# The half swap of q moved to ScalarE's queue, and a longer filler for the last attention head

## The chip, the cores and the metric

The kernel runs on one core of a Trainium2 chip. Its measure is the time of one execution on the device in microseconds (us). The engines are TensorE (PE; its weight loads are listed as PEld), VectorE (DVE), ScalarE (ACT), GpSimd (POOL) and SyncE (SP). Each works through its own list of instructions in order, and semaphores tie the lists together. DMAs are issued from the lists of SyncE, ScalarE and GpSimd.

## The reference

The model is a two-layer (DEPTH = 2) diffusion backbone on 512 latent tokens and 256 context tokens of width 1024, in float32. Each layer projects the normalised tokens with one wide matrix `w_in`, mixes them in three branches, and adds a feed-forward network with a width-3 convolution:

```
z = modulate(rmsnorm(x, norm1_g), sh1, sc1) @ w_in            # 512 + 256 tokens
a: v = layernorm(gelu(z[V]));  y_a = gelu(z[U]) * (w_s @ v + b_s)      # spatial gating, 4 halves of 128 columns each
b: q, k = rope(rmsnorm(z[Q])), rope(rmsnorm(z[K]))            # 8 heads, two maps of 64 dims each
   p = softmax(q0 k0^T) - lam * softmax(q1 k1^T);  y_b = rmsnorm(p @ v)
c: y_c = gb * dwconv3(gc * xin)                                # short convolution
x = x + g1 * ((g_a*(y_a @ wa) + g_b*(y_b @ wb) + g_c*(y_c @ wc)) @ wo)
x = x + g2 * conv_ffn(modulate(rmsnorm(x), sh2, sc2))
```

In layer 0 latent and context tokens are both carried on (768 tokens, attention of the context among itself). In layer 1 the context gives keys and values alone, and everything else runs on the 512 latent tokens.

## The kernel before, in words

Every product with a weight matrix is split: `x = hi + lo`, with `hi` rounded to TensorE's fast 4-byte format and `lo` the rest, and three matmuls (hi*hi, lo*hi, hi*lo; lines 183, 184 and 186, in `gemm`) add up in PSUM. Tokens lie along the free dimension, in segments of 512 and (layer 0) 256. A weight tile of 128 x 1024 is called a half. `Stream` brings the halves in the order in which they are asked for: a load on SyncE's queue (line 62, `wraw`, two buffers), the rounding on ScalarE (line 83, `whi`), the remainder on VectorE (line 69, `wlo`). While the attention runs, `late` is set: `wlo` is not issued with `whi` but by `tick`, after each step of the weave.

The order of the instructions is written out by Python generators. `weave` takes several of them, each with a stated total cost; each yield gives the cost of the step, and the generator whose done share of its total is smallest goes next (ties to the first). So a total that is larger than the sum of the yields makes a generator run ahead of the other one and end early; a total equal to the sum spreads it over the other's whole length.

**One head.** `project(h)` computes q, k and v of head h, normalises q and k and applies the rotation. `turn(h)` then weaves `qk_tr` with one half of filler (`fill(1)`, from `c_fill`) and ends with `v_tr`. `attn(h)` is woven with `project(h + 1)`.

**`qk_tr`** works in three chunks of 256 tokens (in layer 1, k alone in the third). For each chunk it transposes q on TensorE into a PSUM tile (line 738), copies that to `qT[:, 0]` on ScalarE (line 741), and starts two DMAs within SBUF (lines 743 and 744): they copy partitions 0 to 63 of `qT[:, 0]` to partitions 64 to 127 of `qT[:, 1]`, and the other way round. q and k are stored as hi and lo parts above each other (64 + 64 partitions), so that with the swapped copy two matmuls give all four products of the parts. Then it does the same for k: transposes (line 738), and two copies by ScalarE to `kT[0]` and `kT[1]` (line 747). The PSUM pool `mm` has four buffers during the attention; the transposes' tiles, the filler's accumulators and `v_tr`'s tiles take turns in them.

**`scores`** (line 857) multiplies one block of 128 tokens of q with all keys, for both maps a: first `qT[:, 0]` (v = 0), then `qT[:, 1]` (v = 1). VectorE takes the minima (lines 861 and 864, `mn`), ScalarE the exponentials (line 869, `pa`), which also frees the score's PSUM buffer; there are two of these, so the next block's map a waits for this block's exponential of map a. `combine` (VectorE) joins the two maps, `to_at` transposes them (line 893) and splits them into `ah` (ScalarE, line 897) and `al` (VectorE, line 898), and `av` (lines 905 to 907) multiplies with v; ScalarE copies the result to `yb` (line 908). `attn_costs` states 20,000 for these steps in layer 0 and 16,000 in layer 1.

**The last head** has no next projection. It is woven with `fill(99)`: what is left of `c_fill`. The nine halves of branch c are used up by then, so this is the `N_VS` = 2 halves of the gating branch's v, each with yields of 2.6 per token and quarter (7,987 in layer 0, 5,325 in layer 1), with a stated total of `(1 + N_VS) * 10000` (layer 0) or `* 6000` (layer 1). They are only copied out to SBUF (line 842, tags B0 and B7).

**After the attention** `branch_a` is woven with `subln` (totals `62000 - 7800 * N_VS` and 20,000):

```
for v in vg: nc.scalar.activation(v[:, :n], v[:, :n], AF.Gelu_apprx_tanh)   # line 1058
for i in range(N_VS, 4): pv = self.fm(("vs", l, i)); ... Gelu ...; yield 7800  # line 1063
ugate(0); yield 7800          # a half of u on TensorE, gelu on ScalarE
... transposes of vg, layer norm ...; ugate(1); yield 7800
for g in range(4): ... mixing with w_s ...; if g + 2 < 4: ugate(g + 2); yield 7800
```

`subln` first squares five heads (ScalarE line 953, hi part line 170, lo part on VectorE line 171; yield 3700), then sums the eight heads' squares on TensorE (line 968, yield 700 each, squaring three more heads on the way), reads the sums on VectorE (line 973, `srs`, yield 1500), and transposes them on TensorE (line 977) for the reciprocal root (yield 3500).

Of the kernel before, what the change touches and what calls it, by code (L numbers as in the profile page):

```python
# [11 lines left out]
F32 = mybir.dt.float32  # L12
# [8 lines left out]
NL, NC, T, D = 512, 256, 768, 1024  # L21
# [9 lines left out]
N_HALF = 2 * (NH * 3 + 12 + 4 + 4 + 24 + 8 + 8 + 8 + 44 + 24)  # L31
N_ADA = 4 * 24
N_LAST = 3
N_VS = 2


def weave(*gens, tick=lambda: None):
    act = [[g, 0.0, float(tot)] for g, tot in gens]
    while act:
        act.sort(key=lambda e: e[1] / e[2])  # L40
        e = act[0]
        try:
            e[1] += next(e[0])
        except StopIteration:
            act.remove(e)
        tick()
# [83 lines left out]
class Net:  # L130
# [34 lines left out]
    def tick(self, n):  # L165
        for _ in islice(self.bg, n):
            pass
# [555 lines left out]
    def qk_tr(self, l, h, pool, st):  # L723
        nc = self.nc
        qT = pool.tile([128, 2, 2, T], F32R, tag="qT", bufs=1, name="qT")
        kT = [self.slots.tile([128, T], F32R, tag=f"B{1 + a}", name="kT") for a in range(2)]
        y = self.qk_rope(l, 2, pool, st)
        yield 1500
        for c in range(3):
            qs, ks = st.pop(("rope", c))  # L730
            t0 = c * 256
            for v, src in enumerate((qs, ks)):
                if src is None:
                    continue
                pt = self.mm.tile([128, 512], F32R, tag="mm", name="mmT")
                for a in range(2):
                    for b in range(2):
                        nc.tensor.transpose(pt[:, (2 * a + b) * 128:(2 * a + b + 1) * 128], src[:, 2 * b + a, :], self.identr)
                pf = pt.bitcast(F32)
                if v == 0:  # L740
                    nc.scalar.copy(qT[:, 0, :, t0:t0 + 256], pf.rearrange("p (a t) -> p a t", a=2))
                    for i, j in ((0, 64), (64, 0)):
                        nc.sync.dma_start(qT[i:i + 64, 1, :, t0:t0 + 256].bitcast(F32),
                                          qT[j:j + 64, 0, :, t0:t0 + 256].bitcast(F32))
                else:
                    for a in range(2):
                        nc.scalar.copy(kT[a][:, t0:t0 + 256], pf[:, 256 * a:256 * a + 256])
            if c == 0:
                st["rope", 2] = self.qk_hl(*y, pool)
            yield 1700  # L750
        st["q"], st["k"] = qT, kT
# [44 lines left out]
    def c_fill(self, l, pool, scr):  # L796
        nc = self.nc
        segs = self.segs
        n = sum(s[1] for s in segs)
        pc = self.pc[l]  # L800

        def half(b, i, evac, kind="c", mid=None):
            w = self.ws.take(kind, l, b, i) if kind == "c" else self.ws.take(kind, l, i)
            for o, m, _ in segs:
                ps = self.mm.tile([128, 512], F32, tag="mm", name="mm")
                for q in range(4):
                    self.gemm(w, [2 * q, 2 * q + 1], self.h, ((o, m, 0),), (ps,), first=(q == 0), last=(q == 3))
                    if mid and q == 2:
                        mid((o, m, 0))
                    if q == 3:  # L810
                        if o == segs[-1][0]:
                            self.ws.ahead()
                        evac(o, m, ps)
                    yield 2.6 * m

        def mul(dst):
            def f(o, m, ps):
                nc.vector.tensor_tensor(dst[:, o:o + m], dst[:, o:o + m], ps[:, :m], ALU.mult)
            return f

        ps = self.cp

        def first(i):
            ps[i] = self.slots.tile([128, T], F32, tag="B7", name="cp")
            return half(1, i, lambda o, m, q: nc.scalar.copy(ps[i][:, o:o + m], q[:, :m]))

        for i in range(4):
            if i > 1:
                yield first(i)
            if i:  # L830
                yield half(2, i, mul(ps[i]))
            c = pool().tile([128, T], F32, tag="cc", bufs=1, name="cc")

            def conv(seg):
                self.conv(c, ps[i], [pc[:, PC_CW + 4 * j + i:PC_CW + 4 * j + i + 1] for j in range(3)], None, [seg])
            yield half(0, i, mul(c), mid=conv)
            nc.sync.dma_start(scr[i][:, :n], c[:, :n])
        self.vg = []
        for i in range(N_VS):
            v = self.slots.tile([128, T], F32, tag=("B0", "B7")[i], name="vg")  # L840
            self.vg.append(v)
            yield half(0, i, lambda o, m, q: nc.scalar.copy(v[:, o:o + m], q[:, :m]), "vs")

# [202 lines left out]
    def branch_a(self, l, pool):  # L1046
# [10 lines left out]
        for v in vg:  # L1057
            nc.scalar.activation(v[:, :n], v[:, :n], AF.Gelu_apprx_tanh)
        for i in range(N_VS, 4):
            pv = self.fm(("vs", l, i))  # L1060
# [190 lines left out]
    def run(self):  # L1251
        tc, nc, d = self.tc, self.nc, self.d
# [8 lines left out]
        def run(g):  # L1261
            for _ in g:
                pass

        with tc.tile_pool(name="const", bufs=1) as const, tc.tile_pool(name="w", bufs=1) as wp, \
# [45 lines left out]
            for l in range(2):  # L1311
# [12 lines left out]
                with tc.tile_pool(name="attn", bufs=1) as ap, tc.tile_pool(name="pmm", bufs=4, space=PSUM) as self.mm, \  # L1324
                        tc.tile_pool(name="ps", bufs=2, space=PSUM) as self.sp:
                    self.ws.late = True
                    st = [dict(h=h) for h in range(8)]
                    tick = self.ws.low

                    def fill(count):  # L1330
                        while count:
                            g = next(cgen, None)
                            if g is None:
                                return
                            yield from g
                            count -= 1

                    chalf = 7800 if l == 0 else 5200

                    def project(h):  # L1340
                        yield from self.qk_proj(l, h, ap, st[h])
                        vp = self.v_proj(l, h, ap, st[h])
                        yield next(vp)
                        if l:
                            st[h]["kc"]()
                            yield next(vp)
                        if h == 0:
                            self.attn_lam(l, ap, tabs[0])
                        self.qk_norm(l, h, ap, st[h])
                        yield next(vp)  # L1350
                        yield next(vp)
                        y = self.qk_rope(l, 0, ap, st[h])
                        yield next(vp)
                        st[h]["y1"] = self.qk_rope(l, 1, ap, st[h])
                        st[h]["rope", 0] = self.qk_hl(*y, ap)
                        yield next(vp)
                        st[h]["rope", 1] = self.qk_hl(*st[h]["y1"], ap)
                        yield from vp

                    def turn(h):  # L1360
                        weave((self.qk_tr(l, h, ap, st[h]), 6800), (fill(1), chalf), tick=tick)
                        run(self.v_tr(l, h, ap, st[h]))

                    p0 = project(0)
                    for i in range(8):
                        if gb:
                            next(gb)
                        next(p0)
                        tick()
                        if i == 5:  # L1370
                            self.attn_setup(l, ap, *tabs)
                    weave((p0, 15000), (fill(1), chalf), tick=tick)
                    turn(0)
                    for h in range(8):
                        a = self.attn(l, h, ap, st[h]), sum(self.attn_costs(l))
                        if h < 7:
                            weave(a, (project(h + 1), 23500), tick=tick)
                            turn(h + 1)
                        else:
                            weave(a, (fill(99), (1 + N_VS) * (6000 if l else 10000)), tick=tick)  # L1380
                self.ws.low()
                self.ws.late = False
                mmp = psum_all()
# [3 lines left out]
                with tc.tile_pool(name="yk", bufs=16) as yk:  # L1387
# [8 lines left out]
                    with tc.tile_pool(name="tmpa", bufs=1) as tmp:  # L1396
                        pp = PP(tmp)
                        weave((self.branch_a(l, pp), 62000 - 7800 * N_VS), (self.subln(l, pp), 20000))
                    with tc.tile_pool(name="tmpb", bufs=1) as tmp:
# [171 lines left out]
```

## Time and profile before

| | us |
|---|---|
| median of 3 runs | 2674.5 (2672.96 to 2675.52) |
| profiled execution | 2675.01 |
| its span, first to last instruction | 2673.2 |
| TensorE busy | 2617.0 (98% of the span) |
| VectorE busy | 1631.2 (61%) |
| ScalarE busy | 1035.2 (39%) |
| mean granted clock of TensorE | 0.993 of 2.4 GHz |

The profile is of one execution. Matmuls overlap, and their ends are modelled, so a busy TensorE may still lose time between matmuls. A wait is put down to whatever was finished last. Start times in the rows below are microseconds from the start of the span. In a timeline row that stands for several instructions, the time is from the first one's start to the last one's end.

### The profile page before, as it was taken

To read this page: it belongs to the slowest core of one execution; us is meant where nothing else is said; L and a number is where in the kernel's file an instruction comes from. 1 tells how busy PE (TensorE), PEld (TensorE's weight loads), DVE (VectorE), ACT (ScalarE), POOL (GpSimd) and SP (SyncE) were. 2 spreads that over 40 slices of the span, in tenths; PEclk is the share of its full clock that TensorE was granted. 3 is DMA by queue.
4 is the path that set the end of the run, shared out by engine and by line. 5 is a ranking of instruction groups with operands and counts; after the bars stand their busy time and mean duration, and the time that the engine had idled before them with its cause. 6 is when DMAs were issued, how large, how long until landed. Compare 5 with 4: busy or idle time off the path is not lost.

```text
span 2673.2 us, 37362 instructions
## 1 busy us (share of the span) xinstructions
PE 2617.0 (98%) x15128; PEld 2267.7 (85%) x15128; DVE 1631.2 (61%) x2887; ACT 1035.2 (39%) x1840; POOL 220.9 (8%) x202
## 2 busy tenths in 40 slices
PE   7999999999999999999999999999999999999999
PEld 3899999888888888888888878898978888888887
DVE  5677777656546447544544567777767564654544
ACT  3455555542121224312312335555563232343422
POOL 0000000001111111100100100000001121010101
PEclk8999999999999999999999999999999999999999
DMA  5212221224333332222222232212125554233233
GB/s 224 82 44 58 64 66 44 66 66 149 113 116 111 103 127 66 76 87 72 79 81 77 91 100 67 68 55 63 53 75 173 175 163 175 71 99 100 94 103 110
DMA packets 79660, 254.36 MB, mean 95 GB/s; under 512 B 9200, under 2 KB 19712, under 8 KB 79104
## 3 DMA queue, kind: packets, MB, share of 16 engines
q1 hardware_dynamic: 64512, 196.64, 23.1%
q0 software_dynamic: 14544, 55.07, 6.4%
q8 instruction: 119, 1.95, 0.3%
q14 instruction: 53, 0.43, 0.1%
q10 hardware_dynamic: 432, 0.27, 0.0%
HBM read 234.63 MB, written 6.82 MB: 90 GB/s over the span
## 4 chain that ended last, share of the span: by engine, by line
PE 82%; DVE 10%; ACT 4%; DMA 2%; issue 1%; SPq 0%; POOL 0%; ACTq 0%; POOLq 0%; DVEq 0%
PE mm L183 22%; PE mm L186 22%; PE mm L184 22%; PE S L857 3%; PE mm L647 2%; PE mm L649 2%; PE mm L648 2%; DVE wlo L69 2%; PE mmT L893 1%; ACT whi L83 1%; DMA qT<-qT 1%; ACT pa L869 1%; DVE zs L697 1%; DVE al L898 1%; PE mmT L906 1%
## 5 line engine op out<-in xcount | busy, mean ns | idle before, releaser
L183 PE MATMUL mm<-hh,whi 128*128 128x512 f32 (+1 forms) x2392 | 855.3, 358 | 12.1 <-ACT hh L376 10.2
L184 PE MATMUL mm<-hl,whi 128*128 128x512 f32 (+1 forms) x2392 | 820.0, 353 | 4.4 <-DVE hl L379 4.1
L186 PE MATMUL mm<-hh,wlo 128*128 128x512 f32 (+1 forms) x2392 | 752.6, 353 | 1.6 <-DVE wlo L69 1.6
L183 PEld LDWEIGHTS mm<-hh,whi 128*128 128x128 f32 x2392 | 452.6, 189 | 104.5 <-ACT hh L376 14.4
L69 DVE TENSOR_TENSOR wlo<-wraw,whi 128x1024 fp32r<-128x1024 f32 x320 | 399.4, 1249 | 195.8 <-ACT whi L83 194.2
L184 PEld LDWEIGHTS mm<-hl,whi 128*128 128x128 f32 x2392 | 453.3, 190 | 68.4 <-DVE hl L379 9.3
L186 PEld LDWEIGHTS mm<-hh,wlo 128*128 128x128 f32 x2392 | 415.1, 190 | 42.1 <-DVE wlo L69 3.7
L83 ACT CAST whi<-wraw 128x1024 fp32r<-128x1024 f32 x320 | 335.0, 1048 | 285.0 <-PE mm L184 243.4
L1018 DVE SCALAR_TENSOR_TENSOR cv<-mm,pc,cv 128x511 f32<-128x511 f32 (+1 forms) x132 | 86.8, 658 | 181.7 <-ACT cv L1017 180.8
L869 ACT ACTIVATE pa<-S,mn 128x768 f32<-128x768 f32 (+1 forms) x160 | 129.3, 813 | 153.1 <-DVE mn L864 125.7
L183 PE MATMUL mm<-ah,whi 128*128 128x512 f32 (+1 forms) x528 | 187.9, 356 | 0.0
L647 PE MATMUL mm<-whi,hh 128*128 128x256 f32 x640 | 183.0, 286 | 1.3 <-DVE cp L794 0.8
L648 PE MATMUL mm<-wlo,hh 128*128 128x256 f32 x640 | 180.7, 282 | 0.0
L649 PE MATMUL mm<-whi,hl 128*128 128x256 f32 x640 | 180.6, 282 | 0.0
L184 PE MATMUL mm<-al,whi 128*128 128x512 f32 (+1 forms) x528 | 179.9, 354 | 0.0
L186 PE MATMUL mm<-ah,wlo 128*128 128x512 f32 (+1 forms) x528 | 161.7, 355 | 0.0
L1017 ACT ACTIVATE cv<-mm,pc 128x512 f32<-128x512 f32 (+1 forms) x132 | 88.7, 705 | 177.2 <-PE mm L186 177.2
L1179 DVE SCALAR_TENSOR_TENSOR x<-mm,mod,x 128x512 f32<-128x512 f32 (+1 forms) x91 | 58.2, 659 | 139.0 <-PE mm L186 139.0
L1222 POOL TENSOR_TENSOR cv<-cv 128x768 f32<-128x768 f32 (+1 forms) x44 | 91.9, 2088 | 607.3 <-DVE cv L1020 420.7
L857 PE MATMUL S<-kT,qT 128*128 128x512 f32 x576 | 118.2, 341 | 10.1 <-DMA qT<-qT 8.7
L647 PEld LDWEIGHTS mm<-whi,hh 128*128 128x128 f32 x640 | 121.9, 190 | 4.3 <-ACT cp L792 1.0
L864 DVE TENSOR_REDUCE mn<-S 128x1 f32<-128x768 f32 x128 | 116.1, 949 | 10.3 <-PE S L857 10.3
(237 smaller groups left out, 4035.9 us busy)
## 6 DMA issues: line engine op xcount, KB each, us to landing
wraw<-w SPq DMA_DIRECT2D x320, 512.0 KB, 3.6
araw<-ada POOLq DMA_DIRECT2D x80, 512.0 KB, 4.0
qT<-qT SPq DMA_DIRECT2D x80, 128.0 KB, 3.8
araw<-ada SPq DMA_DIRECT2D x16, 512.0 KB, 8.3
x<-xT SPq DMA_DIRECT2D x8, 384.0 KB, 7.7
srow<-sscr POOLq DMA_DIRECT2D x3, 1024.0 KB, 5.5
x<-xT POOLq DMA_DIRECT2D x8, 384.0 KB, 6.2
xscr<-x SPq DMA_DIRECT2D x8, 256.0 KB, 3.9
```

Source lines behind the costliest of these rows:

```text
L69: self.lo_eng.tensor_tensor(lo, raw, hi.bitcast(F32), ALU.subtract)
L83: self.nc.scalar.copy(hi, raw)
L183: nc.tensor.matmul(ps[:, :m], lhsT=hh, rhs=xh[:, o:o + m], start=st, stop=False)
L184: nc.tensor.matmul(ps[:, :m], lhsT=hh, rhs=xl[:, o:o + m], start=False, stop=False)
L186: nc.tensor.matmul(ps[:, :m], lhsT=hl, rhs=xh[:, o:o + m], start=False, stop=sp)
L647: nc.tensor.matmul(ps[:, :256], lhsT=hh[:, sl], rhs=hi[:, c:c + 256], start=(k == 0), stop=False)
L648: nc.tensor.matmul(ps[:, :256], lhsT=hh[:, sl], rhs=lo[:, c:c + 256], start=False, stop=False)
L649: nc.tensor.matmul(ps[:, :256], lhsT=hl[:, sl], rhs=hi[:, c:c + 256], start=False, stop=(k == 7))
L857: nc.tensor.matmul(s[:, c0 + o:c0 + o + m], lhsT=st["q"][:, v, a, t0:t0 + 128], rhs=st["k"][a][:, k0 + o:k0 + o + m], start=(v == 0), stop ...
L864: nc.vector.tensor_reduce(mn[:, a:a + 1], ss[a], AX.X, ALU.min)
L869: nc.scalar.activation(pa[:, :nk], ss[a], AF.Exp, bias=mn[:, a:a + 1], scale=-1.0, accum_out=sm[a])
L1222: nc.gpsimd.tensor_tensor(cs[1][:, :n], cs[1][:, :n], cs[0][:, :n], ALU.mult)
```

## The change

The two DMAs of the swap are issued from ScalarE's queue and not from SyncE's. A third half of the gating branch's v goes into the last head's filler (and into slot B2, which holds `kT[1]` before) and leaves `branch_a`. The filler's stated total is set to `N_VS * 10.4` per token, which is the sum of its yields: 23,962 in layer 0 and 15,974 in layer 1. Since `branch_a`'s total depends on `N_VS`, that falls from 46,400 to 38,600.

```diff
-N_VS = 2
+N_VS = 3
...
                 if v == 0:
                     nc.scalar.copy(qT[:, 0, :, t0:t0 + 256], pf.rearrange("p (a t) -> p a t", a=2))
                     for i, j in ((0, 64), (64, 0)):
-                        nc.sync.dma_start(qT[i:i + 64, 1, :, t0:t0 + 256].bitcast(F32),
-                                          qT[j:j + 64, 0, :, t0:t0 + 256].bitcast(F32))
+                        nc.scalar.dma_start(qT[i:i + 64, 1, :, t0:t0 + 256].bitcast(F32),
+                                            qT[j:j + 64, 0, :, t0:t0 + 256].bitcast(F32))
                 else:
                     for a in range(2):
                         nc.scalar.copy(kT[a][:, t0:t0 + 256], pf[:, 256 * a:256 * a + 256])
...
         for i in range(N_VS):
-            v = self.slots.tile([128, T], F32, tag=("B0", "B7")[i], name="vg")
+            v = self.slots.tile([128, T], F32, tag=("B0", "B7", "B2")[i], name="vg")
...
-                            weave(a, (fill(99), (1 + N_VS) * (6000 if l else 10000)), tick=tick)
+                            weave(a, (fill(99), N_VS * 10.4 * (512 if l else 768)), tick=tick)
```

## Rows read from the trace of the kernel before

**Rows 1.** From the page: busy time in us, share of the span and instructions of each engine.

```profile
PE 2617.0 (98%) x15128; PEld 2267.7 (85%) x15128; DVE 1631.2 (61%) x2887; ACT 1035.2 (39%) x1840; POOL 220.9 (8%) x202
```

**Rows 2.** The view of waits, TensorE alone, over the whole span: who waited for whom, us in total, times, longest.

```profile
PE S L857 <- DMA qT<-qT: 8.7, 7, 1.5
...
PE mmT L905 <- ACT ah L897: 4.3, 3, 3.2
...
PE mmT L738 <- ACT qT L741: 1.5, 3, 0.5
```

**Rows 3.** Single lines of the kernel. The first two are of the swap (line 743): length of an issue in ns (min/median/max), first and last start, and then us from issue to landing. The next is of the loads of `pc` (line 1287), which ScalarE's queue issues. The last two are ScalarE's timeline at the start of the program (start us, us, engine, line, operation): a DMA issue and the instruction behind it.

```profile
L743 SPq DMA_DIRECT2D qT<-qT x80: 590/605/1403, 117.1 to 1957.0; - x80
...
DMA to landing us min/median/max: 2.3/3.8/5.5
...
L1287 ACTq DMA_DIRECT2D pc<-pcol x2: 335/335/335, 7.1 to 8.3; - x2
...
0.74 0.41 ACTq L1269 DMA_DIRECT2D cc<-cc  x1
...
1.18 1.28 ACT L1271 ACT_TABLE_LOAD   x1 [1.18 <-PEq L1566]
```

**Rows 4.** Timeline of one turn of layer 1 (head 6), SyncE's queue and then TensorE: start us, us, engine, line, operation, out<-in, form, count, and in brackets the engine's idle time before and what ended it.

```profile
1909.26 0.33 SPq L62 DMA_DIRECT2D wraw<-w  x1
...
1909.77 2.57 SPq L743 DMA_DIRECT2D qT<-qT  x4
...
1915.08 1.29 PE L857 MATMUL S<-kT,qT 128*128 128x512 f32 x6 [1.04 <-DMA qT<-qT]
```

**Rows 5.** Timeline of one turn of layer 0, ScalarE: the copies of q and k of the three chunks, the split of the next weight half, and the exponentials of the first two score steps.

```profile
378.55 0.58 ACT L741 CAST qT<-mmT 128x512 fp32r<-128x512 f32 x1
...
379.02 0.66 ACT L747 CAST kT<-mmT 128x256 fp32r<-128x256 f32 x2
...
381.06 0.41 ACT L716 CAST qs<-ry 128x256 fp32r<-128x256 f32 x1 [1.38 <-DVE ry L708]
...
382.15 0.65 ACT L747 CAST kT<-mmT 128x256 fp32r<-128x256 f32 x2
...
383.64 0.69 ACT L747 CAST kT<-mmT 128x256 fp32r<-128x256 f32 x2
...
384.17 1.10 ACT L83 CAST whi<-wraw 128x1024 fp32r<-128x1024 f32 x1
...
388.64 0.90 ACT L869 ACTIVATE pa<-S,mn 128x768 f32<-128x768 f32 x1 [1.68 <-DVE mn L864]
...
393.61 0.90 ACT L869 ACTIVATE pa<-S,mn 128x768 f32<-128x768 f32 x1 [1.89 <-DVE mn L864]
```

**Rows 6.** The same turn of layer 0: one row of VectorE (the minima of the first score step) and three of TensorE (k's transposes of the third chunk, the second and the third score step).

```profile
387.66 1.81 DVE L864 TENSOR_REDUCE mn<-S 128x1 f32<-128x768 f32 x2
...
382.86 0.54 PE L738 MATMUL mmT<-identr,ks 128*128 128x128 f32 x4
...
390.41 1.57 PE L857 MATMUL S<-kT,qT 128*128 128x512 f32 x8
...
394.68 1.83 PE L857 MATMUL S<-kT,qT 128*128 128x512 f32 x8
```

**Rows 7.** Line 738 (the transposes of q and k), whole span, from its list of what TensorE's weight loads and matmuls waited for there: releaser, us, times. The second row is ScalarE's timeline of the first turn of layer 0.

```profile
  ACT kT L747: 1.2, 8
...
123.14 0.86 ACT L780 CAST vh<-mmT 128x512 fp32r<-128x512 f32 x2 [1.07 <-PE mmT L778]
```

**Rows 8.** Timeline of the turn of Rows 4 and of the score steps behind it: ScalarE, VectorE, TensorE.

```profile
1910.12 0.41 ACT L719 CAST ks<-ry 128x256 fp32r<-128x256 f32 x1 [0.83 <-DVE ry L708]
...
1912.14 1.06 ACT L83 CAST whi<-wraw 128x1024 fp32r<-128x1024 f32 x1
...
1916.72 0.90 ACT L869 ACTIVATE pa<-S,mn 128x768 f32<-128x768 f32 x1 [2.35 <-DVE mn L864]
...
1921.69 0.90 ACT L869 ACTIVATE pa<-S,mn 128x768 f32<-128x768 f32 x1 [1.89 <-DVE mn L864]
...
1915.74 1.81 DVE L864 TENSOR_REDUCE mn<-S 128x1 f32<-128x768 f32 x2
...
1919.08 1.57 PE L857 MATMUL S<-kT,qT 128*128 128x512 f32 x8
...
1923.35 1.56 PE L857 MATMUL S<-kT,qT 128*128 128x512 f32 x8
```

**Rows 9.** Busy time by stretch (stretch, its length, then each engine's busy us with its instructions, granted clock, DMA share and GB/s): the end of the last head of layer 0 and of layer 1.

```profile
519.00:530.00 11.00, 6.51 (x35) 5.26 (x33) 5.56 (x15) 4.10 (x13) 0.64 (x2) 0.84 0.16 48
...
1981.50:1987.50 6.00, 4.44 (x31) 3.70 (x30) 2.01 (x5) 2.91 (x7) 0.74 (x2) 1.00 0.30 90
```

**Rows 10.** Timeline behind the attention: for layer 0 ScalarE's gelu of a gating half straight from TensorE, VectorE's low part of the first square, and VectorE's reading of the sums of squares; for layer 1 the gelu and the low part of the first square.

```profile
538.17 0.87 ACT L1063 ACTIVATE vg<-mm 128x512 f32<-128x512 f32 x2 [4.87 <-issue]
...
540.68 0.96 DVE L171 TENSOR_TENSOR sql<-ssq,sqh 128x768 fp32r<-128x768 f32 x1 [5.72 <-ACT sqh L170]
...
560.61 1.01 DVE L973 TENSOR_SCALAR srs<-ssum 8x512 f32<-8x512 f32 x2 [4.75 <-PE ssum L968]
...
1992.51 0.60 ACT L1063 ACTIVATE vg<-mm 128x512 f32<-128x512 f32 x1 [2.49 <-issue]
...
1994.31 0.69 DVE L171 TENSOR_TENSOR sql<-ssq,sqh 128x512 fp32r<-128x512 f32 x1 [2.63 <-ACT sqh L170]
```

## The prediction, made before the result was known

> **What bounds the kernel now.** I read the page first: TensorE is busy for 2617.0 of 2673.2 us [rows 1], so only 56 us are to be had, and what the other engines do counts only where TensorE waits for it. The view of waits then shows the three places that the change touches: seven waits for the swap's DMA, 8.7 us in all; four waits behind `ah` and `qT`, where the attention's own chain is late [rows 2]. Third I took the timelines of one turn in each layer, to see who has slack. In layer 1 SyncE issues a 512 KB weight load at 1909.26 and the four swap DMAs from 1909.77 on, behind it in one queue; the scores with `qT[:, 1]` go on only at 1915.08, 5.3 us after the first issue [rows 4], against a shortest landing of 2.3 [rows 3]. In layer 0 nothing waits for the swap. There the list of line 738 shows eight waits for the k copies (`kT`), one for each of the eight turns [rows 7]: the third chunk's k transposes need the PSUM buffer of the second chunk's. In the turn shown the copies end at 382.15 + 0.65 = 382.80 and the transposes start at 382.86 [rows 5, 6]. So ScalarE has no slack in layer 0's turns.
>
> **Part 1: the swap on ScalarE's queue.** Removed: SyncE's 80 issues. SyncE's other work (weight loads, stores of `cscr`) is not held up by them at present, so that gives nothing. Added: 80 issues in ScalarE's list, two behind each q copy, each waiting for that copy to end; queued behind them are the k copies, the filler's evacuations, the next `whi`, `vh` and the exponentials.
>
> The price of one issue on ScalarE stands in no row for this shape. From above: the same DMA holds SyncE 605 ns. From below on ScalarE: a DMA of another shape takes 335 ns [rows 3]. Below that still: nothing, if ScalarE's engine went on with its next copy meanwhile. A row speaks against nothing: the table load starts at 1.18, right behind the end at 0.74 + 0.41 = 1.15 of an issue ahead of it [rows 3], but that is one case. I take 605 ns, since the shape is the same: a pair costs 2 x 0.605, about 0.1 for two semaphores and gaps, and 0.11 by which the k copy overlaps the q copy now (379.13 against 379.02 [rows 5]): 1.4 us a chunk.
>
> The Trainium skill, "Perfetto Trace Analysis", section "DMA Instruction — HWDGE (DVE, Sync)", has the issuing sequencer free for its next instruction only when the descriptors are generated, and the profiled time cover just that. By it the sum is the one below; by an issue that blocks nothing it would be rival C. One row agrees, none settles it.
>
> *Layer 0, the turn shown.* First chunk: ScalarE idles 1.38 before 381.06 [rows 5], which absorbs the 1.4. Second chunk: the k copies move from 382.15 to 383.6, so TensorE's third k transposes move from 382.86 to 384.3, and TensorE with them: +1.4. Third chunk: the k copies are late by both pairs, 383.64 to 386.4, and so `whi`, 384.17 to 387.0. From there the chain is VectorE's `wlo`, `vl`, the minima (387.66 to 390.4 [rows 6]) and the exponentials, 388.64 to 391.4. The first exponential ends at 389.54 and the second score step starts at 390.41: slack 0.87. TensorE arrives there at 391.8 and waits until 392.3: +1.9. The same chain runs on through the next weight split to the next exponential, 393.61 + 0.90 = 394.51, and the third score step starts at 394.68: slack 0.17. So that step is late by 2.8 - 0.17, 2.6 us, and TensorE never gets it back. In the first turn ScalarE idles another 1.07 before `vh` [rows 7]: 1.7. Layer 0: 7 x 2.6 + 1.7 = 20 us. With 335 ns an issue a chunk is 0.85 (0.67 + 0.07 + 0.11): 7 x 1.5 + 0.7 = 11. With issues that block nothing: 0.
>
> *Layer 1, the turn shown.* Two chunks swap. ScalarE idles 0.83 before 1910.12 [rows 8], so 0.6 of the first pair and 1.4 of the second remain: `whi` 1912.14 to 1914.1. I let 0.4 of these 2.0 be absorbed before the minima (no row here for it): they start at 1917.3 rather than 1915.74, the exponential at 1918.3 rather than 1916.72, ending at 1919.2. The swap, issued a microsecond earlier and no longer behind the load, has landed by the time of the scores, so TensorE saves its wait, about 1.3 with what is lost around the 1.04, less 0.5 because k's third transposes come later. It reaches the second score step at 1918.3, waits until 1919.2, and is where it was (1919.08). The next exponential ends at 1921.69 + 0.90 + 1.6 = 1924.2, and the third score step starts then instead of at 1923.35: +0.85. Eight heads: 7 us slower. What is late next is thus the exponential, in the place of the DMA. Bounds: -10 (seven waits of 8.7 in all, with the restart, go and nothing comes) and +13 (1.6 a head).
>
> **Part 2: the filler.** TensorE's work stays: the third half has as many matmuls in the filler as in `branch_a`. Now the filler's two halves are used up at 15,974 of a stated 30,000, about half-way, and the attention's end runs bare. In layer 0 TensorE idles 11.00 - 6.51 = 4.5 us there, and the granted clock is 0.84, part of the stretch at 1.2 GHz, some 1.5 us more; in layer 1 it idles 1.6 [rows 9]. With filler up to the last step both go, but for the copy of the last accumulator, 0.5 each: -5.5 and -1. The thinner filler (1.8 pieces a step in layer 0 for 2.25, 1.1 for 1.3 in layer 1) leaves the early score steps less cover; I put +1 on that.
>
> But `branch_a` loses what it gives. With a total of 38,600 its one remaining v half counts 7,800/38,600 = 0.202, more than the 3,700/20,000 = 0.185 of `subln`'s first yield, so the first sum of squares now follows at once on the half, behind which the squares are only started: in ScalarE's order they stand behind the half's gelu. In layer 0 that gelu starts at 538.17 and the first low part ends at 540.68 + 0.96 = 541.64: TensorE waits 3.6, where now a whole half covers it. Layer 1: 1992.51 to 1995.0, so 2.5 [rows 10]. And the sums (`srs`, 1.01 [rows 10]) now stand right between the last sum and their transposes: +1.3 and +1. Costs 4.9 and 3.5, gains 5.5 and 1, thinner filler 1: +3 us. Bounds: -6.5 (all of the cover kept) and +9 (the bare end replaced by other waits).
>
> **Sum.** On the profiled execution's 2675.0 (span 2673.2, 1.8 around it): 20 + 7 + 3 = 30, so 2705. The median shown is 0.5 lower: 2704.
>
> **Rivals.**
> *B: the issue is cheaper.* 335 ns as in ScalarE's own row [rows 3]. Layer 0 +11; in layer 1 only 0.85 is left of a hold, the DMA waits go and the exponentials stay within their slack of 1919.08 - 1917.62: -8; filler +3. 2675 + 6, so 2681.
> *C: faster. ScalarE's engine goes on while its queue issues.* Then no k copy is late, the seven waits of rows 2 and the restarts go (-10), and with +3 for the filler the time is 2668; with a filler that costs nothing 2665. For it: 8.7 us are really there, and ScalarE is busy 39% of the time. Against: the table load that starts on the issue's heels. It decides at the first pair: if the k copy behind an issue starts before the issue's end, C holds.
> *D: nothing moves.* The swap's transfers still share the DMA engines with the weight load and land as late as now (up to 5.5 [rows 3]), and the issues are small enough for ScalarE's idle times. Then only the filler's +3: 2678. Against: the swap alone has landed in 2.3. The Trainium skill, "DMA: Bandwidth & Descriptors", section "Issuing engines are not separate DMA queues", says that transfers interleave on the same 16 engines whoever starts them, and that another issuer saves only issue time, small beside the transfer; this is that rule, and the late landing of rows 4 goes with it, the 1.2 us a pair do not look small here.
>
> **How the numbers follow.** Forecast A 0.60 (2692 to 2712, from 1.7 to 2.8 a turn in layer 0 and from 0 to +13 in layer 1), B 0.10, C 0.22, D 0.08. This kernel's runs tell 0.2%, 5.3 us, from no change: faster is below 2669, slower above 2680. C lies below that bound with 0.16 and within with 0.06; D within with 0.05 and above with 0.03; B above: faster 0.16, same 0.11, slower 0.73. The range goes from 2666 to 2712: it leaves out the lower half of C and the upper end of A.
>
> **What would show it.** On the path: ScalarE's timeline in a layer 0 turn with two issues of about 0.6 between q copy and k copy, and k copies 1.4 later (C: no delay). TensorE's waits for `kT` at line 738 grow from 1.2 to over 10 us, those for `pa` at line 857 from 1.4 to over 10, those for the swap's DMA vanish. One layer 0 head takes 2.6 longer. Behind the attention TensorE waits for `sql` once in each layer, 2.5 to 3.6 us; the idle time of rows 9 is gone. The forecast is wrong if an issue takes under 0.3 or blocks nothing, or if the score steps keep their distance to the exponentials.

## The result, and the profile after

The changed kernel takes 2710.3 us (median of four runs, 2709.5 to 2710.8) against 2675.0 for the kernel before beside it: a ratio of 1.0133, 95% interval 1.0119 to 1.0147, so 35 us slower. The forecast was 2704, slower, with a range of 2666 to 2712.

The page of the kernel after: busy time and share of the span (2708.9 us) by engine, and the engines' shares of the chain that ended last.

```profile
PE 2631.9 (97%) x15128; PEld 2274.4 (84%) x15128; DVE 1630.8 (60%) x2887; ACT 1036.6 (38%) x1842; POOL 220.4 (8%) x202
...
PE 74%; DVE 13%; ACT 8%; DMA 2%; ACTq 2%; issue 1%; SPq 0%; DVEq 0%
```

TensorE is 14.9 us busier than in [rows 1] with the same 15,128 matmuls. The other 20.8 of the span's 35.7 us are idle time. Part of the 14.9 is the clock: the mean granted clock fell from 0.993 to 0.990 over the span, which is some 8 us at full speed (an estimate from these rounded figures: 0.010 x 2708.9 less 0.007 x 2673.2). `ACTq`, ScalarE's issuing, now has 2% of the chain. The waits tell where TensorE stood (TensorE alone, whole span: us in total, times, longest).

```profile
PE S L857 <- ACT pa L869: 14.5, 26, 1.8
...
PE mmT L738 <- DVE ks L720: 4.4, 7, 1.5
...
PE ssum L968 <- ACT sqh L170: 4.3, 2, 2.4
PE ssum L977 <- DVE srs L973: 4.1, 2, 2.8
PE mmT L738 <- DVE cc L818: 4.1, 3, 1.4
PE mmT L738 <- ACT kT L747: 2.9, 2, 1.5
...
PE S L857 <- DMA qT<-qT: 0.2, 1, 0.2
```

The swap's own wait has gone from 8.7 to 0.2 us [rows 2]. In its place the score steps wait 14.5 us for the exponentials, k's transposes wait for ScalarE's copies and for VectorE's `ks` and `cc`, and behind the attention there are two new waits for squares and two for sums.

The list of the swap after (length of an issue in ns, first and last start; us to landing):

```profile
L743 ACTq DMA_DIRECT2D qT<-qT x80: 597/616/1748, 115.4 to 1983.4; - x80
...
DMA to landing us min/median/max: 2.3/2.5/5.6
```

An issue costs ScalarE 616 ns, where SyncE paid 605 [rows 3]. The landing is better, 2.5 for 3.8, but these are medians over both layers; in layer 1, where every swap meets a weight load, it is 3.6 for 4.3. The turn of [rows 5, 6] after the change, ScalarE and then TensorE:

```profile
393.15 0.59 ACT L741 CAST qT<-mmT 128x512 fp32r<-128x512 f32 x1
393.77 1.27 ACTq L743 DMA_DIRECT2D qT<-qT  x2
395.08 0.65 ACT L747 CAST kT<-mmT 128x256 fp32r<-128x256 f32 x2 [1.34 <-PE mmT L738]
...
402.72 0.90 ACT L869 ACTIVATE pa<-S,mn 128x768 f32<-128x768 f32 x1 [2.05 <-DVE mn L864]
...
407.69 0.90 ACT L869 ACTIVATE pa<-S,mn 128x768 f32<-128x768 f32 x1 [1.88 <-DVE mn L864]
```

```profile
395.78 0.53 PE L738 MATMUL mmT<-identr,ks 128*128 128x128 f32 x4 [1.45 <-ACT kT L747]
...
403.76 0.50 PE L857 MATMUL S<-kT,qT 128*128 128x512 f32 x1 [0.30 <-ACT pa L869]
...
408.74 0.85 PE L857 MATMUL S<-kT,qT 128*128 128x512 f32 x3 [0.26 <-ACT pa L869]
```

The k copy begins at 395.08, behind the end of the pair of issues at 395.04. The bracket behind it ("1.34 <-PE") names TensorE, but the row above shows ScalarE's own queue in that time. TensorE pays twice: 1.45 us before the third k transposes, and then from these to the third score step 408.74 - 395.78 = 12.96 instead of 394.68 - 382.86 = 11.82 [rows 6], another 1.14. Together 2.6 us in this turn.

### The profile page after: what moved, and what is told of

It reads as the page before. It is cut to its first block, busy times and chain, and to the rows that moved or that the text cites. A ratio compares the mean times of both kernels' runs of the same rounds, so it can differ in the third digit from the quotient of the medians.

```text
span 2708.9 us, 37309 instructions
## 1 busy us (share of the span) xinstructions
PE 2631.9 (97%) x15128; PEld 2274.4 (84%) x15128; DVE 1630.8 (60%) x2887; ACT 1036.6 (38%) x1842; POOL 220.4 (8%) x202
## 4 chain that ended last, share of the span: by engine, by line
PE 74%; DVE 13%; ACT 8%; DMA 2%; ACTq 2%; issue 1%; SPq 0%; DVEq 0%
PE mm L183 21%; PE mm L186 21%; PE mm L184 21%; PE S L857 2%; DVE wlo L69 2%; ACT whi L83 2%; ACT pa L869 2%; PE mm L647 2%; PE mm L649 2%; PE mm L648 2%; ACTq L743 2%; PE mmT L893 1%; DVE mn L864 1%; ACT kT L747 1%; DMA wraw<-w 1%
## 5 line engine op out<-in xcount | busy, mean ns | idle before, releaser
L857 PE MATMUL S<-kT,qT 128*128 128x512 f32 x576 | 123.3, 348 | 15.0 <-ACT pa L869 14.5
L648 PEld LDWEIGHTS mm<-wlo,hh 128*128 128x128 f32 x640 | 122.1, 191 | 0.9 <-DVE wlo L69 0.8
```

The source lines that it names most:

```text
L648: nc.tensor.matmul(ps[:, :256], lhsT=hh[:, sl], rhs=lo[:, c:c + 256], start=False, stop=False)
L857: nc.tensor.matmul(s[:, c0 + o:c0 + o + m], lhsT=st["q"][:, v, a, t0:t0 + 128], rhs=st["k"][a][:, k0 + o:k0 + o + m], start=(v == 0), stop ...
```

## The experiments

Each is an edit of the kernel before, unless it says otherwise. Changes in us are the ratio's, on 2675; the brackets behind a ratio are its 95% interval.

**The swap alone** (the `nc.scalar.dma_start` lines of the change, nothing else).

> The swap on ScalarE's queue, the filler as before (two halves, old total). Theory (each chunk holds ScalarE for 1.3 us, and the k copies, the weight split and the exponentials behind it end later than TensorE can wait): the forecast's 20 us in layer 0 and 7 in layer 1, so +27, 2702; with the starts of the heads in the changed kernel's trace (layer 0's eight turns +17 to +18, layer 1's +8 to +9) +26. Rival (the loss is the filler's, the swap alone saves its DMA waits): about 2666 to 2675.

2703.2 us, ratio 1.0104 (1.0088 to 1.0119), 28 us. The waits for `pa` at line 857 are 13.3 us.

**The filler alone** (the other lines of the change, the swap on SyncE's queue).

> The third half and the new total, the swap on SyncE's queue as before. Theory by the forecast: +3, 2678. By the changed kernel's trace, where the waits behind the two attentions (first sum of squares, then the sums' transposes) and the clock's fall after them come to some 11 us against 8 gained at the attentions' ends: +3 to +9, 2678 to 2684. Rival (cover is only moved, or the filler gains): 2668 to 2675.

2681.9 us, ratio 1.0028 (1.0018 to 1.0038), 7.5 us; its ten runs spread from 2677.5 to 2688.6. The two parts add up within their intervals: 0.0104 + 0.0028 = 0.0132 for the measured 0.0133. The first mixing with `w_s` (line 1101) is a mark behind the attention and the sums of each layer. Its matmuls before the change, with the swap alone, with the filler alone, and with both (ns min/median/max, first and last start; layer 0, layer 1):

```profile
L1101 PE MATMUL mm<-wst,vt x48: 270/275/377, 572.1 to 595.0; 128*128 128x128 f32 x48
...
L1101 PE MATMUL mm<-wst,vt x32: 270/275/377, 2014.7 to 2030.2; 128*128 128x128 f32 x32
```

```profile
L1101 PE MATMUL mm<-wst,vt x48: 270/275/377, 591.7 to 614.5; 128*128 128x128 f32 x48
...
L1101 PE MATMUL mm<-wst,vt x32: 270/275/377, 2045.1 to 2060.6; 128*128 128x128 f32 x32
```

```profile
L1101 PE MATMUL mm<-wst,vt x48: 272/275/377, 571.8 to 594.6; 128*128 128x128 f32 x48
...
L1101 PE MATMUL mm<-wst,vt x32: 270/275/582, 2020.0 to 2037.6; 128*128 128x128 f32 x32
```

```profile
L1101 PE MATMUL mm<-wst,vt x48: 270/275/377, 590.9 to 613.7; 128*128 128x128 f32 x48
...
L1101 PE MATMUL mm<-wst,vt x32: 270/275/582, 2049.7 to 2067.2; 128*128 128x128 f32 x32
```

By the first mark the swap costs 591.7 - 572.1 = 19.6 us in layer 0; by the second, 30.4, so another 10.8 in layer 1. The filler costs -0.3 and 5.6. The traces with both and with the filler alone give the swap once more: 590.9 - 571.8 = 19.1 us, and 29.7 by the second mark, so another 10.6. (From the second mark to the span's end the four have 658.5, 659.0, 659.3 and 659.2, so little is left out. The swap alone was 2.7 us slower in its profiled execution than in its median, 2705.9 for 2703.2, so its two shares together are up to that much too large.)

**The swap on ScalarE's queue in layer 1 alone.**

```diff
-                        nc.sync.dma_start(qT[i:i + 64, 1, :, t0:t0 + 256].bitcast(F32),
+                        (nc.scalar if l else nc.sync).dma_start(qT[i:i + 64, 1, :, t0:t0 + 256].bitcast(F32),
```

> The swap on ScalarE's queue in layer 1 alone, nothing else changed. Theory: layer 1 has a wait to save (8.7 us in seven waits) and still loses, because the exponential takes the DMA's place: +7 by the forecast, +8 by the trace, 2682 to 2683. Rival (only layer 0, which had no wait for the swap, loses; layer 1 gains what its waits were): 2665 to 2667.

2687.1 us, ratio 1.0046 (1.0031 to 1.0061), 12 us, although the wait for the swap's DMA is gone here too: it is paid back with more for `pa` and, at k's transposes, for `ks` (0.2 before). The rival's gain did not come. TensorE's waits:

```profile
PE S L857 <- ACT pa L869: 9.4, 19, 1.7
...
PE mmT L738 <- DVE ks L720: 4.8, 8, 1.3
```

The listed waits are only part of the 12 us. From layer 1's first transposes to those of its last head, 320.5 us before and 329.8 here, TensorE's idle time grows by 3.5 us and its busy time by 5.8 for the same 2184 matmuls, at the same mean clock of 0.99: much of the loss stands inside the recorded times of matmuls, the score step's (line 857) by 2.6. The two stretches, before and here (length, busy us of TensorE, its weight loads, VectorE, ScalarE, GpSimd; granted clock; DMA):

```profile
1631.20:1951.70 320.50, 310.90 (x2184) 283.88 (x2185) 243.01 (x487) 176.91 (x397) 0.00 (x0) 0.99 0.21 61
...
1631.55:1961.37 329.82, 316.69 (x2184) 284.67 (x2185) 243.00 (x487) 176.12 (x397) 0.00 (x0) 0.99 0.20 59
```

**The swap on GpSimd's queue** (`nc.gpsimd` in its place), which has nothing in its list behind it during a turn.

> The swap issued from GpSimd's queue, nothing else changed: off SyncE's queue and not in ScalarE's way. Theory (the wait of layer 1 comes from the weight load ahead in the same queue, and the loss from ScalarE's time): the seven waits go, nothing comes: -9 to -10, 2665. Rival 1 (the transfers share the DMA engines and land as late as before): 2675. Rival 2 (GpSimd's issues are slower, or wait for VectorE, and land later): 2675 to 2690.

2677.2 us, ratio 1.0002 (0.9992 to 1.0011): nothing. No engine of the path is held, but the swap isn't earlier either: TensorE waits 10.0 us for it at line 857, where it waited 8.7 [rows 2]. In the turn of [rows 4], GpSimd's timeline, SyncE's, and then two DMA views (size of one, median us from issue to landing): the first pair of this turn, and a swap of layer 0 that GpSimd issues at 331.9 us, between two weight loads:

```profile
1910.64 1.17 POOL L743 DMA_DIRECT2D qT<-qT  x2 [42.18 <-ACT qT L741]
```

```profile
1910.88 5.99 SPq L62 DMA_DIRECT2D wraw<-w  x2
```

```profile
qT<-qT POOLq DMA_DIRECT2D x2, 128.0 KB, 5.6
...
qT<-qT POOLq DMA_DIRECT2D x1, 128.0 KB, 2.5
```

GpSimd begins to issue the first pair 0.24 us ahead of the weight load, from another queue, and this pair lands in 5.6 us all the same. GpSimd's queue is not slow by itself: between two loads its swap lands in 2.5 us, 0.2 above the shortest from SyncE's [rows 3]. That fells my expectation that the place in SyncE's queue was what made the swap late, and bears out the rival. The Trainium skill, "DMA: Bandwidth & Descriptors", section "Issuing engines are not separate DMA queues", says that transfers share the same engines whoever issues them; the 5.6 us agree.

**Half the dose**: one DMA of each pair from ScalarE.

```diff
-                        nc.sync.dma_start(qT[i:i + 64, 1, :, t0:t0 + 256].bitcast(F32),
+                        (nc.sync if i else nc.scalar).dma_start(qT[i:i + 64, 1, :, t0:t0 + 256].bitcast(F32),
```

> The kernel before with one of the two DMAs of each swap issued from ScalarE's queue and the other left on SyncE's: half the dose of the swap alone, which cost 26.7 us. Theory (what costs is how long an issue holds ScalarE between the q copy and the k copy): one issue of about 0.62 us instead of a pair of 1.26 a chunk; in layer 0 some 7 x 1.0 to 1.5, in layer 1 the late swap stays for the half that SyncE issues, behind the weight load, and 0.3 to 0.6 a head is added by the hold; +9 to +15 us, TensorE's waits for pa at line 857 between 4 and 10 us in all. Rival 1 (a fixed cost comes with any issue there, such as the wait for the q copy at the head of ScalarE's queue): nearly the whole loss, +22 or more. Rival 2 (ScalarE's slack takes one issue a chunk): within 4 us of before.

2685.5 us, ratio 1.0039 (1.0025 to 1.0053), 10 us: a bit over a third of the loss for half of the issues. The loss grows with the time for which the queue is held, more than in proportion here; a fixed price for any issue is out. With half of the swap still issued by SyncE, its wait in layer 1 stays. TensorE's waits:

```profile
PE S L857 <- DMA qT<-qT: 7.7, 8, 1.6
...
PE S L857 <- ACT pa L869: 3.6, 11, 0.9
```

**The filler with the sums' cover kept** (the filler alone, but `branch_a`'s total left where it was).

```diff
-                        weave((self.branch_a(l, pp), 62000 - 7800 * N_VS), (self.subln(l, pp), 20000))
+                        weave((self.branch_a(l, pp), 62000 - 7800 * 2), (self.subln(l, pp), 20000))
```

> The filler part of the change alone, swap as before, but branch_a's stated total stays 46,400, so that a half of the branch stands again between the squares and the first sum of squares. Without that the filler alone cost 7.5 us. Theory (the bare end of the last head did go, and the loss is the two waits for the low part of the squares, 4.3 us in all, with the clock's fall behind them): the waits for sqh at line 968 go, some of those for srs at line 977 may stay (1 to 3 us); 0 to -6 us against before. Rival (the loss comes from the thinner filler, or from vg's third evacuation, and the cover does not matter): still +5 to +9.

2672.6 us, ratio 0.9989 (0.9980 to 0.9998), 3 us faster (0.5 to 5 by the interval). Against the filler alone one stated number is worth 0.0028 + 0.0011, so about 10 us. There is no wait for `sqh` or `srs` left. Instead TensorE waits for the layer norm's values `vt` (2.0 us at line 1101, 1.3 at line 183).

**Only the spreading** (two halves as before, over their real length).

```diff
-                            weave(a, (fill(99), (1 + N_VS) * (6000 if l else 10000)), tick=tick)
+                            weave(a, (fill(99), N_VS * 10.4 * (512 if l else 768)), tick=tick)
```

> Only the spreading of the filler: two halves as before, over their stated real length (10.4 a column), no third half; the swap as before. Theory (the bare end of the last head is what costs, and branch_a keeps its cover since nothing is taken from it): layer 0's idle end of 4.5 us is partly filled, for the price of thinner filler in the early score steps; -1 to -4 us, and no wait for sqh at line 968. Rival 1 (with two halves the thinner filler leaves as much idle time in the steps as it takes from the end): within 1 us of before. Rival 2 (spreading is what cost the 7.5 us): +4 or more.

2672.7 us, ratio 0.9991 (0.9982 to 0.9999), 2.4 us faster (0.3 to 5 by the interval). So neither the spreading nor the third half cost the 7.5 us; the total that `branch_a` lost with the half did.

**The load behind the swap, first try**: a flag set in `turn` keeps `low` from calling `load_to` until the first chunk's swap is issued.

```diff
...
-        self.load_to(0)
+        if not self.hold:
+            self.load_to(0)
...
+                    if c == 0:
+                        self.ws.hold = False
+                        self.ws.load_to(0)
...
                     def turn(h):
+                        self.ws.hold = True
```

> The aim of the swap's move reached by another way: the swap stays in SyncE's queue, but the weight load that SyncE issues just ahead of it in a turn is held back until the first chunk's two swap DMAs have been issued. Theory (the swap landed late since the load's 512 KB were ahead of it on the shared DMA engines, whichever queue issues): the first chunk's swap lands 2.3 to 3 us after its issue, the seven waits for qT at line 857 (8.7 us) go or fall under 2 us, and the time falls by 5 to 10 us. Rival 1 (the wait is for the second chunk's swap, which the held load then meets): the waits stay above 5 us and the time is within 3 us of before. Rival 2 (the load that comes later is late for its matmuls): new waits for a weight tile, +2 us or more.

2676.2 us, ratio 1.0002 (0.9993 to 1.0010). The edit did not do what it was to do: the load stands in SyncE's list before `turn` begins, and SyncE still issues it first (1910.13, the swaps from 1910.63). The run says nothing on the theory.

**The load behind the swap, second try**: the hold begins at the end of `project`, stops `load_to` itself, and ends behind the second chunk's swap; layer 1 alone.

```diff
...
             i = self.loaded
+            if self.hold and i > self.split:
+                return
...
+                    if c == 1 and l:
+                        self.ws.hold = False
+                        self.ws.load_to(0)
...
+                        self.ws.hold = l > 0
                         yield from vp
```

> The load really held, in layer 1 alone (the run before this one set the hold too late: the load stood in SyncE's list ahead of the swaps already, and the order of its DMAs was that of before). From the last product of the v projection on, SyncE issues no weight load until the four swap DMAs of both chunks are issued. Theory (the swap waits for the load's 512 KB on the shared DMA engines): the swaps land 2.3 to 3.5 us after their issue instead of 4.0 to 4.7, the waits for qT at line 857 fall from 8.7 to under 2 us, and the time falls by 5 to 10 us. Rival 1 (the exponentials set the second score step, as the prediction has it with the swap on ScalarE): the waits for qT go, waits for pa take their place, and the time falls by less than 3 us. Rival 2 (the load that now starts 2.5 us later is late for its copy and matmuls): new waits for whi or wlo, and the time rises.

2671.9 us, ratio 0.9980 (0.9971 to 0.9988), 5.4 us faster. The landing of the swap in layer 1 (all 32, from 1600 to 2000 us), SyncE's timeline in the turn of [rows 4], and TensorE's wait at the score steps (line 862 here):

```profile
DMA to landing us min/median/max: 2.3/2.3/3.6
```

```profile
1905.25 3.52 SPq L745 DMA_DIRECT2D qT<-qT  x4
1908.86 2.88 SPq L64 DMA_DIRECT2D wraw<-w  x2
```

```profile
PE S L862 <- ACT pa L874: 4.3, 13, 0.7
```

The swap lands in a median of 2.3 us, where it took 4.3 in layer 1 before. The waits for it are gone with SyncE issuing it, and no wait for a weight takes their place. Part comes back as waits for `pa`, 4.3 us for 1.4 before; 8.7 - 2.9 = 5.8 us is about what was measured. (The trace alone has less: by the same matmuls as the marks above, line 1106 here, at 571.4 and 2010.3 us, layer 1 gains 3.7.)

**The held load with each of the two good fillers.**

> The held load together with the filler of two halves spread over its real length (that alone: -2.3 us). The two touch different stretches, so by the theory the gains add: -7 to -12 us against before, and 2.3 below the held load alone. If the held load gives nothing: -2.

> The held load together with the third half in the filler and the half kept between the squares and the first sum (that alone: -2.4 us). By the theory the gains add: -7 to -12 us against before. If the held load gives nothing: -2.

2670.0 us, ratio 0.9970 (0.9959 to 0.9981), with the spread filler; 2668.5 us, ratio 0.9969 (0.9956 to 0.9981), with the third half and the cover. Both are 8 us faster, as they should be if the gains add; the intervals, some 3 us to each side, do not show it to better than that, and the two are not told apart. Both beat the kernel before and the kernel after.

## Why the prediction was right

**The issue blocks ScalarE, at SyncE's price: right.** 605 ns was taken, 616 ns came, and the k copy starts 0.04 us after the pair's end. Rivals B and C fall by that. The half dose is the test by experiment.

**Layer 0, 20 us: the mechanism right, the size in part by luck.** The turn shown loses the 2.6 us that were worked out, by the two steps that were named: the third k transposes are late by 1.45 (1.4 forecast), the third score step by another 1.14 (1.2). With the swap alone the layer loses 19.6. But this turn does not stand for all. From one turn's first transposes to those of the next, the swap alone adds 1.7, 2.8, 2.6, 1.7, 2.8, 2.6 and 1.7 us, and the last turn adds 1.3: 17 in eight turns, where 20 were forecast. In turns 1, 4 and 7 the third k transposes do not wait as they do in the other five (`kT` twice and `cc` three times in the view above); the forecast had a cheaper turn only in the first. The other 2.7 us come behind the attention, where TensorE's granted clock is 0.50 (its level of 1.2 GHz) for 10.2 us in that execution. The kernel after has two stretches of 3.4 us at this level in its turns, behind the waits at the third k transposes of turns 5 and 8; the trace before has 1.00 from 100 to 520 us. The forecast had no term for the clock. The first row is of the swap alone, the second of the kernel after (stretch, length, busy us of TensorE, its weight loads, VectorE, ScalarE, GpSimd; granted clock; DMA):

```profile
541.60:551.80 10.20, 9.28 (x33) 7.64 (x32) 2.10 (x4) 5.28 (x8) 1.07 (x2) 0.50 0.18 51
...
341.70:345.10 3.40, 3.40 (x18) 3.40 (x17) 1.29 (x3) 1.99 (x4) 0.00 (x0) 0.50 0.33 80
```

One of the signs named was wrong: the waits for `kT` were to grow from 1.2 to over 10 us. In the list of line 738, which counts weight loads and matmuls (the 1.2 were of weight loads), they grow to 6.1; for the matmuls alone the view has 2.9, in two turns of layer 0. In three more turns there the same wait is put down to VectorE's `cc` (4.1). The 4.4 for `ks` are of layer 1. Neither was in the forecast. The waits for `pa`, "over 10", are 14.5.

**Layer 1, 7 us: the mechanism right, the size low.** The term "0.85 a head" measured about 1.3 (10.8 / 8 with the swap alone; 12 us in the run of layer 1 alone). It stays under the bound of 13. Here too one turn was taken for eight: the turn shown loses 1.0, close to the forecast, but from turn to turn the swap alone adds 0.0, 1.9, 0.6, 1.9, 2.0, 1.0 and 1.2 us. The turn of [rows 8] after the change, ScalarE and then TensorE:

```profile
1933.11 0.60 ACT L741 CAST qT<-mmT 128x512 fp32r<-128x512 f32 x1
1933.74 1.26 ACTq L743 DMA_DIRECT2D qT<-qT  x2
...
1943.04 0.90 ACT L869 ACTIVATE pa<-S,mn 128x768 f32<-128x768 f32 x1 [2.33 <-DVE mn L864]
```

```profile
1944.09 0.49 PE L857 MATMUL S<-kT,qT 128*128 128x512 f32 x1 [0.67 <-ACT pa L869]
...
1949.06 0.50 PE L857 MATMUL S<-kT,qT 128*128 128x512 f32 x1 [0.25 <-ACT pa L869]
```

Both score steps now wait for an exponential, as the forecast had it: what is late next is `pa`. Why some heads lose twice as much I did not separate. That there was a gain to be had, and that the hold on ScalarE outweighed it, is shown by the held load: with the swap landing early and ScalarE free, the kernel is faster, by 5.4 and not by the whole 8.7 us.

**The filler, 3 us: the term mis-sized.** Layer 0's sum came out as worked (-5.5 and +4.9 forecast, -0.3 measured). Layer 1's "3.5" for `branch_a` was too low. Windows after the change: the end of the last head in layer 0, and a stretch at each of three waits (stretch, length, busy us of TensorE, its weight loads, VectorE, ScalarE, GpSimd; granted clock):

```profile
533.50:548.50 15.00, 15.00 (x106) 13.84 (x105) 6.30 (x14) 6.79 (x17) 0.47 (x1) 1.00 0.11 36
...
563.60:567.00 3.40, 3.40 (x12) 2.92 (x11) 2.10 (x3) 3.33 (x5) 0.00 (x0) 0.50 0.00 0
...
2027.90:2031.30 3.40, 3.18 (x8) 2.50 (x9) 1.93 (x4) 3.33 (x6) 0.00 (x0) 0.50 0.05 18
...
2048.50:2055.20 6.70, 6.02 (x21) 5.23 (x22) 4.39 (x20) 0.33 (x1) 1.62 (x2) 0.50 0.26 78
```

The bare end of layer 0 is filled (15.00 of 15). And TensorE at those waits, then VectorE ahead of the last of them:

```profile
561.47 0.62 PE L968 MATMUL ssum<-sqh,zsel 128*128 128x512 f32 x2 [2.44 <-ACT sqh L170]
...
2027.40 0.50 PE L968 MATMUL ssum<-sqh,zsel 128*128 128x512 f32 x1 [1.85 <-ACT sqh L170]
...
2049.18 0.59 PE L977 MATMUL ssum<-ident,srs 8*128 8x8 f32 x4 [2.79 <-DVE srs L973]
```

```profile
2045.49 1.91 DVE L1092 TENSOR_SCALAR vt<-vt,mv,rsy 128x512 f32<-128x512 f32 x4
2047.32 1.22 DVE L69 TENSOR_TENSOR wlo<-wraw,whi 128x1024 fp32r<-128x1024 f32 x1
2048.45 0.67 DVE L973 TENSOR_SCALAR srs<-ssum 8x512 f32<-8x512 f32 x1
```

The squares cost 2.4 and 1.9 us, with 0.6 in all for their low parts (line 171) behind, less than the 3.6 and 2.5 forecast; the wait is for the high part `sqh` and not, as the sign said, for `sql`. The step that failed is "the sums (`srs`) now stand right between the last sum and their transposes: +1.3 and +1". In layer 0 that held: 4.1 in all less 2.8 leaves 1.3. In layer 1 `srs` stands in VectorE's list behind the layer norm and a `wlo`: 2.79, not 1. And I left out what comes with a wait: TensorE's granted clock is 0.50 for 3.4 us behind the first two of them, and for 6.7 from the end of the last one on; the kernel before has 1.00 from 530 to 600 and from 1990 to 2020 us. At half speed 3.4 us lose at most 1.7, and 6.7 at most 3.4. So layer 0's sum is partly luck: the squares came cheaper, and the clock, which was not in the forecast, can have taken that back. In layer 1 only 1.2 us of the last stretch lie ahead of the mark at 2049.7. Up to there the terms are 1.9 + 2.8 + 1.7 + 0.6 at most, less 1 for the bare end, so 6 against the 5.6 measured. What gave back most of the rest, up to 2.8 behind the mark, I did not settle; these are single executions, and the trace before has a stretch of 3.4 us at 0.50 at 1633.9 which the filler alone does not have.

**The sum.** 27 for the swap and 3 for the filler were forecast, 28 and 7.5 came. The forecast of 2704 is 6 us short, 4.5 of them the filler's. That the swap's 27 came so close is partly luck, since layer 0's turns lost less than forecast and layer 1's more. (The "four waits behind `ah` and `qT`" are six in [rows 2], three of each; nothing was worked out from them.)

**Rival D, by its mechanism, half true.** On GpSimd's queue the transfers did share the engines with the load, and nothing moved. On ScalarE's queue too the load slows them, and what counts is who comes first. In the turn above, the first DMA is issued at 1933.74, 0.49 us ahead of the load (1934.23), and the second 0.15 behind it. Their landing, one after the other (size of each, us from issue to landing):

```profile
qT<-qT ACTq DMA_DIRECT2D x1, 128.0 KB, 2.4
...
qT<-qT ACTq DMA_DIRECT2D x1, 128.0 KB, 4.6
```

Of layer 1's eight turns, the first DMA lands in 2.4 to 2.5 us in five and in 4.0 to 5.6 in three; the second takes 4.3 to 5.3 in all. What cost the time was the issue.

## What to carry to other kernels

A DMA issue is an instruction in the list of the engine that issues it, here of 0.6 us for a swap (0.33 for a weight load [rows 4]): price it by who stands behind it there, not by that engine's busy share. When a small transfer is late behind a large one, turn their order round at the issue; another queue helps only as far as it brings the small one ahead (half a microsecond on ScalarE's queue did so in five turns of eight, 0.24 us on GpSimd's did not in the turn shown). Work out more than one turn before you multiply: here the turns lost between 0.0 and 2.8 us each. And when a step is taken out of a stretch whose order follows from stated totals, look at which covers move: here one stated number was worth about 10 us.

## What was not expected of the hardware

GpSimd pays nearly the same for an issue of this DMA (1.17 us a pair) as ScalarE (1.26). A pair whose issue begins 0.24 us ahead of a 512 KB load's, on another queue, is still slowed by it, to 5.6 us. And at the waits of 1.9 to 2.8 us that TensorE has behind the attention, 3.4 to 6.7 us at a granted clock of 0.50 follow.
